# Shift and scale of the first norm: all four quarters of w_ada as matmul weights with two moving columns

## Chip, core and metric
One core of one Trainium2 chip. The metric is the device time of one execution in microseconds (us); of the kernel before, three runs took 3079.60, 3080.01 and 3080.32. Engines are named as in the profile: PE (TensorE matmul), PEld (its weight loads), DVE (VectorE), ACT (ScalarE), POOL (GpSimd), SP (SyncE, which here issues most transfers).

## What is computed
A block with attention, a gated linear recurrence and a convolutional feed-forward on 512 tokens of width 1024 with 256 context tokens, then four further layers. The change concerns its first lines:

```python
mod = jax.nn.silu(c) @ w_ada[layer] + b_ada[layer]
mod_c = jax.nn.silu(c_ctx) @ w_ada[layer] + b_ada[layer]
sh1, sc1, gt1, sh2, sc2, gt2 = jnp.split(mod[:, None, :], 6, axis=-1)
sh1c, sc1c, gt1c, sh2c, sc2c, gt2c = jnp.split(mod_c, 6, axis=-1)
h = modulate(rms_norm(x_lat, norm1_g[layer]), sh1, sc1)
hc = modulate(rms_norm(x_ctx, norm1_g[layer]), sh1c, sc1c)
```

with `modulate(h, shift, scale) = h * (1 + scale) + shift`. The projections q, kv and so on take `h` and `hc`.

## The kernel before
**Layout.** Activations lie with the channel on the partitions: eight blocks of 128 channels (KD = 8) by 512 tokens, and 256 more columns for the context. A shift or a scale is thus one column of 128 values for each block; `m01` holds them as [128, 8 blocks, token or context, shift or scale]. Inputs are fp32. Large products are made of three: weights and activations are split into a rounded high part and a rest (`whi`, `wlo`, `xh`, `xl`), and `mm3` issues high by high, high by rest and rest by high (lines 202, 203, 204).

**Where the work is.** `norm1` (from line 400) is the first stage of the program. `w_ada01` is the part of w_ada for shift and scale, stored as four quarters of 2 MB: quarter 0 is the shift of blocks 0 to 3, quarter 1 the scale of the same, quarter 2 shift and scale of blocks 4 and 5, quarter 3 of blocks 6 and 7. Each comes in two transfers (`adaw`, four buffers), each with four of the eight 128-row blocks of the contraction.

- *Quarters 0 and 1* (`ada`, `columns`). The weights of the array are the two silu vectors padded with zeros to 32 columns (`s2`), and the moving operand is w_ada, 512 columns: eight fp32 products a quarter (line 441) give a 32x512 row, ACT copies it out (444), and eight transposes (452) bring the rows into columns. DVE then adds the bias or scales (456 to 458).
- *Quarters 2 and 3* (`fetch`, `sums`). For each of the two vectors a weighted sum over the eight blocks is built on 128x512 tiles (`adas`): for the tokens on DVE (476), for the context by ACT (478) and POOL (479). Then a product with a column of ones sums over the partitions (483), 128x2 each.
- *The factors* (`factors`). The squares of x are summed over the blocks (292, 295 on ACT, 298 on DVE), `inv_rms` sums over the partitions (223) and makes 1/rms on DVE, `spread` makes a row of it over all partitions with two products (264), and ACT copies that out (266).
- *The products* (`first`). For each block k, x times the factor (502: two blocks on DVE, six on POOL), then `operand`: `xh` on ACT (508), a second copy `u` and the rest `xl` on DVE (510, 512, 513), both by the block's columns in `m01`; then 15 products of 512 columns into five banks (two for kv, three for q). Eight blocks make 120. The context follows with 48 products of 256 columns. After these come two panels `gq`, 24 products each, the first of them mixed in with the context before.

**What sets the order.** The program is written as one sequence. A scheduler then places the instructions, and each engine runs its own list in the order that it made; an engine that waits holds up all behind it. The places of the `next(...)` calls only suggest the order. SP issues transfers in its list's order too, and a raw panel (`wraw`) has three buffers.

`group` issues a row of matmuls as one accumulation in a bank:

```python
        ops = [self.nc.tensor.matmul(*o, start=i == 0, stop=i == last) for i, o in enumerate(ops)]
        for i in range(1, last + 1):
            self.after(ops[0], ops[i])
```

Of the kernel before, what the change touches and what calls it, by code (L numbers as in the profile page):

```python
# [155 lines left out]
class K:  # L156
# [214 lines left out]
    def silu_c(self, pool):  # L371
        nc = self.nc
        self.s2 = pool.tile([P, KD, 32], F32, name="s2")
        nc.vector.memset(self.s2, 0.0)
        nc.scalar.activation(self.s2[:, :, 0], self.v("c", 0, 8), AF.Silu)
        nc.scalar.activation(self.s2[:, :, 1], self.v("c_ctx", 0, 8), AF.Silu)
# [23 lines left out]
    def norm1(self, psp, psf, psb, evict_q, then):  # L400
# [3 lines left out]
        with self.pool(name="n1", bufs=1) as pool:  # L404
# [3 lines left out]
            def first(k):  # L408
# [10 lines left out]
                for t, a, b in ((0, 0, 256), (1, 256, 640)):  # L419
# [8 lines left out]
            row = self.wp.tile([P, PANEL], F32, tag="wraw", name=self.nm("row"),  # L428
                               bufs=self.raw_bufs)[:32, :].rearrange("p (q c) -> p q c", q=2)

            def ada(q):

                ps = psp.tile([P, 512], F32, tag="mm", name=self.nm("ps"))
                for h in range(2):
                    raw = pool.tile([P, 4, 512], F32, tag="adaw", name=self.nm("adaw"), bufs=4)
                    nc.sync.dma_start(raw, A["w_ada01"][q, h])
                    for k in ((range(4), range(4, 6)), (range(6, 8), ()))[q][h]:
                        nc.sync.dma_start(xa[:, k, :T], A["xa"][k, :, :T])
                    for i in range(4):
                        k = 4 * h + i  # L440
                        nc.tensor.matmul(ps[:32, :], self.s2[:, k, :], raw[:, i, :], start=k == 0, stop=k == KD - 1)
                    if h == 0:
                        yield 1
                nc.scalar.copy(row[:, q, :], ps[:32, :])
                yield 1

            def columns():

                for k in range(4):
                    for j in range(2):  # L450
                        o = (k * 2 + j) * 32
                        nc.tensor.transpose(fl[:, o:o + 32], row[:, j, k * P:(k + 1) * P], self.ident[:32, :32])
                f = fl[:, :256].rearrange("p (k j c) -> p k j c", j=2, c=32)
                cols = lambda v: v.rearrange("p (k o) -> p k o", o=1).to_broadcast([P, 4, 2])
                sc = m01[:, :4, :, 1]
                nc.vector.tensor_tensor(sc, f[:, :, 1, :2], cols(g[:, :4]), ALU.mult)
                nc.vector.tensor_tensor(sc, sc, cols(bg[:, :4]), ALU.add)
                nc.vector.tensor_tensor(m01[:, :4, :, 0], f[:, :, 0, :2], cols(self.v("b_ada", 0, 4)), ALU.add)

            def fetch(p):  # L460

                raws = []
                for h in range(2):
                    raws.append(pool.tile([P, 4, 512], F32, tag="adaw", name=self.nm("adaw"), bufs=4))
                    nc.sync.dma_start(raws[h], A["w_ada01"][p, h])
                return raws

            def sums(p, i, raws):

                t = pool.tile([P, 512], F32, tag=f"adas{i}", name=self.nm("adas"), bufs=2)  # L470
                for k in range(KD):
                    r, f = raws[k // 4][:, k % 4, :], self.s2[:, k, i:i + 1]
                    if k == 0:
                        nc.scalar.mul(t, r, f)
                    elif i == 0:
                        nc.vector.scalar_tensor_tensor(t, r, f, t, ALU.mult, ALU.add)
                    else:
                        nc.scalar.mul(r, r, f)
                        nc.gpsimd.tensor_tensor(t, t, r, ALU.add)
                yield 1  # L480
                o = 384 + ((p - 2) * 2 + i) * 8
                for c in range(4):
                    nc.tensor.matmul(fl[:, o + 2 * c:o + 2 * c + 2], t[:, c * P:(c + 1) * P], self.ones[:, 0:2],
                                     start=True, stop=True)
                ks = slice(2 * p, 2 * p + 2)
                sc = m01[:, ks, i, 1]
                nc.vector.tensor_tensor(sc, fl[:, o + 4:o + 8:2], g[:, ks], ALU.mult)
                nc.vector.tensor_tensor(sc, sc, bg[:, ks], ALU.add)
                nc.vector.tensor_tensor(m01[:, ks, i, 0], fl[:, o:o + 4:2], self.v("b_ada", 2 * p, 2), ALU.add)
# [25 lines left out]
            for _ in ada(0):  # L515
                pass
            a1 = ada(1)
            next(a1)
            r = factors(0, T)
            next(a1)  # L520
# [5 lines left out]
            raws = [fetch(2)]  # L526
            pans = [next(wf[0])]
            columns()
            next(wf[2])
            pkv = [psb.tile([P, 1024], F32, tag="big", name=self.nm("ps")) for _ in range(2)]  # L530
            pq = [psp.tile([P, 512], F32, tag="mm", name=self.nm("ps")) for _ in range(3)]
            for k in range(KD):
# [11 lines left out]
                if k == 0:  # L544
                    c2 = sums(2, 0, raws[0])
                    next(c2)
                    raws.append(fetch(3))
                    t2 = sums(2, 1, raws[0])
                    next(t2)
# [1245 lines left out]
```

## Time and profile before
| what | value |
|---|---|
| median of 3 runs | 3080.01 us |
| profiled execution | 3079.63 us |
| its span, first to last instruction | 3077.8 us |
| PE busy, share of the span | 2989.1 us, 97% |
| DVE, ACT, POOL busy | 70%, 48%, 17% |
| mean granted PE clock | 0.987 |
| chain that ended last | PE 78%, DVE 7%, ACT 2%, issue 2%, POOL 1% |

The profiled execution takes 1.83 us more than its span. The chain is followed back from the last instruction to what released it at each step. Busy matmuls overlap: a record's duration is longer than the distance to the next, so costs are read from the distance between starts. An fp32 product stands as two records, one of `xh` and its like as one. The granted clock is a share of 2.4 GHz; the levels met are 1.00 and 0.50.

### The profile page before, as it was taken

The page shows a single profiled execution, that of the slowest core. Times are in us where ns is not written, and L with a number is a line of the kernel's source. Part 1 is how long each engine was busy: PE and PEld are TensorE (multiplying, and loading weights), DVE is VectorE, ACT ScalarE, POOL GpSimd, SP SyncE. Part 2 cuts the span into 40 slices and gives each one's busy share as a digit, 9 for nine tenths or more (in the row PEclk, how much of TensorE's full clock was granted, in tenths as well). Part 3 has the DMA queues.
Part 4 walks back from the last instruction along what each step waited for, and adds up shares of the span by engine and source line. Part 5 has one row for each costly group of instructions (what it writes and reads, how often), then busy time and mean ns, then how long its engine had stood idle before and what let it go on. Part 6 is the DMA issues. An engine that isn't in the chain of part 4 may idle for free.

```text
span 3077.8 us, 42669 instructions
## 1 busy us (share of the span) xinstructions
PE 2989.1 (97%) x16044; PEld 2566.1 (83%) x16044; DVE 2159.4 (70%) x3596; ACT 1475.9 (48%) x2429; POOL 508.8 (17%) x453
## 2 busy tenths in 40 slices
PE   7999999989999999999999999999999999999998
PEld 4878778778888778999888999888899987789997
DVE  7858795689953985666845677765566788756766
ACT  5336653443333664444544445532444466644544
POOL 3212310110001211111201111210211122111112
PEclk8999999999999999999999999999999999999999
DMA  5671233523333435667524666623566654357664
GB/s 203 195 240 53 83 111 109 199 90 96 97 94 99 123 92 156 160 166 171 139 93 127 163 166 161 145 95 97 145 162 168 166 127 125 97 156 171 159 168 107
DMA packets 164271, 421.08 MB, mean 137 GB/s; under 512 B 18241, under 2 KB 24769, under 8 KB 163041
## 3 DMA queue, kind: packets, MB, share of 16 engines
q1 hardware_dynamic: 118000, 334.91, 34.5%
q0 software_dynamic: 36864, 67.13, 13.5%
q10 hardware_dynamic: 9200, 16.32, 1.6%
q8 instruction: 126, 2.06, 0.3%
q14 instruction: 81, 0.66, 0.1%
HBM read 398.10 MB, written 13.63 MB: 134 GB/s over the span
## 4 chain that ended last, share of the span: by engine, by line
PE 78%; DVE 7%; ACT 2%; issue 2%; POOL 1%; DMA 0%; SPq 0%; POOLq 0%; DVEq 0%; ACTq 0%
PE ps L334 20%; PE ps L202 18%; PE ps L204 18%; PE ps L203 18%; DVE wlo L188 1%; DVE xc L1264 1%; PE po L223 1%; DVE wlo L285 1%; PE pu L928 0%; DVE xc L1338 0%; PE pt L811 0%; DVE tg L1336 0%; PE ps L223 0%; ACT whi L186 0%; DVE x L1189 0%
## 5 line engine op out<-in xcount | busy, mean ns | idle before, releaser
L202 PE MATMUL ps<-xh,whi 128*128 128x512 f32 x2224 | 873.7, 394 | 11.4 <-ACT xh L508 6.6
L204 PE MATMUL ps<-xh,wlo 128*128 128x512 f32 x2224 | 873.1, 393 | 5.4 <-DVE wlo L188 4.6
L203 PE MATMUL ps<-xl,whi 128*128 128x512 f32 x2224 | 872.5, 392 | 3.1 <-DVE xl L513 3.1
L186 ACT CAST whi<-wraw 128x1024 fp32r<-128x1024 f32 (+2 forms) x267 | 265.1, 995 | 549.2 <-PE ps L203 383.7
L334 PE MATMUL ps<-hh,whi 128*128 128x256 f32 x1792 | 511.1, 285 | 5.1 <-DVE x L1189 5.1
L334 PE MATMUL ps<-hl,whi 128*128 128x256 f32 x1792 | 508.0, 283 | 0.0
L334 PE MATMUL ps<-hh,wlo 128*128 128x256 f32 x1792 | 504.2, 283 | 0.0
L202 PEld LDWEIGHTS ps<-xh,whi 128*128 128x128 f32 x2224 | 420.8, 189 | 99.7 <-ACT xh L508 6.8
L204 PEld LDWEIGHTS ps<-xh,wlo 128*128 128x128 f32 x2224 | 420.6, 189 | 96.6 <-DVE wlo L188 7.4
L203 PEld LDWEIGHTS ps<-xl,whi 128*128 128x128 f32 x2224 | 421.0, 189 | 90.1 <-DVE xl L513 4.6
L188 DVE TENSOR_TENSOR wlo<-wraw,whi 128x1024 fp32r<-128x1024 f32 (+2 forms) x257 | 300.2, 1168 | 186.9 <-ACT whi L186 185.4
L279 ACT CAST whi<-wraw 128x512 fp32r<-128x512 f32 (+2 forms) x400 | 232.7, 612 | 366.0 <-PE ps L203 231.6
L105 POOL DMA_DIRECT2D s<-in_w x256 | 223.9, 1038 | 1053.2 <-ACT s L116 513.5
L334 PEld LDWEIGHTS ps<-hh,whi 128*128 128x128 f32 x1792 | 343.4, 192 | 10.3 <-ACT whi L279 3.5
L334 PEld LDWEIGHTS ps<-hl,whi 128*128 128x128 f32 x1792 | 343.6, 192 | 0.7
L334 PEld LDWEIGHTS ps<-hh,wlo 128*128 128x128 f32 x1792 | 342.4, 192 | 0.0
L285 DVE TENSOR_TENSOR wlo<-wraw,whi 128x512 fp32r<-128x512 f32 (+2 forms) x400 | 264.1, 686 | 19.5 <-ACT whi L279 11.3
L1189 DVE TENSOR_TENSOR x<-x,ps 128x256 f32<-128x256 f32 x448 | 185.0, 417 | 114.8 <-PE ps L334 113.5
L279 ACT CAST whi<-s 128x512 fp32r<-128x512 f32 x256 | 153.4, 617 | 188.9 <-PE ps L334 147.7
L1178 DVE SCALAR_TENSOR_TENSOR H<-ps,rb 128x512 f32<-128x512 f32 x128 | 88.1, 691 | 177.6 <-PE ps L204 174.8
L298 POOL TENSOR_TENSOR acc_x<-acc_x,sq 128x512 f32<-128x512 f32 x54 | 79.2, 1467 | 651.6 <-ACT sq L295 650.9
L285 DVE TENSOR_TENSOR wlo<-s,whi 128x512 fp32r<-128x512 f32 x256 | 178.9, 715 | 10.4 <-ACT whi L279 1.2
(418 smaller groups left out, 4425.9 us busy)
## 6 DMA issues: line engine op xcount, KB each, us to landing
wraw<-in_w SPq DMA_DIRECT2D x192, 512.0 KB, 3.9
s<-in_w POOLq DMA_DIRECT2D x256, 256.0 KB, 6.5
s<-in_w SPq DMA_DIRECT2D x128, 256.0 KB, 5.0
wraw<-in_w_up SPq DMA_DIRECT2D x44, 512.0 KB, 3.4
wraw<-in_a_w_in SPq DMA_DIRECT2D x40, 512.0 KB, 3.5
wraw<-in_w_ada SPq DMA_DIRECT2D x32, 512.0 KB, 4.2
a<-in_w SPq DMA_DIRECT2D x64, 256.0 KB, 5.3
wraw<-in_w_in SPq DMA_DIRECT2D x29, 512.0 KB, 3.7
```

Of the source, the lines that this page charges most:

```text
L105: d = nc.gpsimd.dma_start(t, x, accum_op=ALU.add)
L186: nc.scalar.copy(hi[:, :n], raw[:, :n])
L188: e.tensor_tensor(lo[:, :n], raw[:, :n], hi[:, :n].bitcast(F32), ALU.subtract)
L202: mm(out, wh, xh, start=start, stop=False)
L203: mm(out, wh, xl, start=False, stop=False)
L204: mm(out, wl, xh, start=False, stop=stop)
L279: i = nc.scalar.copy(hi, src)
L285: e.tensor_tensor(lo, src, hi.bitcast(F32), ALU.subtract)
L298: (nc.vector if k == last else eng or nc.gpsimd).tensor_tensor(acc, acc, s, ALU.add)
L334: mm = lambda *o, **kw: self.nc.tensor.matmul(*o, skip_group_check=not start, **kw)
L1178: nc.vector.scalar_tensor_tensor(h, ps, 0.0, self.rb, ALU.max, ALU.mult)
L1189: nc.vector.tensor_tensor(x[:, n, :], x[:, n, :], ps, ALU.add if sign > 0 else ALU.subtract)
```

## The change
All four quarters go one way: w_ada's 128x128 blocks are the weights of the array and the two silu vectors are the moving operand, so that a product gives the 128x2 columns directly. A quarter is 8 x 4 = 32 fp32 products in one group (32 for each p, line 223 in the profile, since `group` records there). `s2` shrinks to two columns without the memset, and `row`, `columns`, `sums` and the tiles `adas` go. Quarters 2 and 3 are placed behind blocks 1 and 3 of the products, and all of `fetch` stands ahead of them.

```diff
-        self.s2 = pool.tile([P, KD, 32], F32, name="s2")
-        nc.vector.memset(self.s2, 0.0)
+        self.s2 = pool.tile([P, KD, 2], F32, name="s2")
...
-            def ada(q):
...
-                    for i in range(4):
-                        k = 4 * h + i
-                        nc.tensor.matmul(ps[:32, :], self.s2[:, k, :], raw[:, i, :], start=k == 0, stop=k == KD - 1)
...
-                nc.scalar.copy(row[:, q, :], ps[:32, :])
-            def columns():
...
-                for k in range(4):
-                    for j in range(2):
-                        o = (k * 2 + j) * 32
-                        nc.tensor.transpose(fl[:, o:o + 32], row[:, j, k * P:(k + 1) * P], self.ident[:32, :32])
...
-            def fetch(p):
+            def fetch(p, xs=((), ())):
...
                 raws = []
                 for h in range(2):
                     raws.append(pool.tile([P, 4, 512], F32, tag="adaw", name=self.nm("adaw"), bufs=4))
                     nc.sync.dma_start(raws[h], A["w_ada01"][p, h])
+                    for k in xs[h]:
+                        nc.sync.dma_start(xa[:, k, :T], A["xa"][k, :, :T])
                 return raws
-            def sums(p, i, raws):
...
-                    if k == 0:
-                        nc.scalar.mul(t, r, f)
-                    elif i == 0:
-                        nc.vector.scalar_tensor_tensor(t, r, f, t, ALU.mult, ALU.add)
-                    else:
-                        nc.scalar.mul(r, r, f)
-                        nc.gpsimd.tensor_tensor(t, t, r, ALU.add)
...
-                    nc.tensor.matmul(fl[:, o + 2 * c:o + 2 * c + 2], t[:, c * P:(c + 1) * P], self.ones[:, 0:2],
-                                     start=True, stop=True)
...
+            def ada(p, raws):
+
+                if p < 2:
+                    o, ps = 0, psp.tile([P, 512], F32, tag="mm", name=self.nm("ps"))
+                else:
+                    o, ps = 384 + 8 * (p - 2), fl
+                self.group([(ps[:, o + 2 * c:o + 2 * c + 2], raws[k // 4][:, k % 4, c * P:(c + 1) * P], self.s2[:, k, 0:2])
+                            for k in range(KD) for c in range(4)])
+                got = ps[:, o:o + 8].rearrange("p (c i) -> p c i", i=2)
+                cols = lambda v, n: v.rearrange("p (k o) -> p k o", o=1).to_broadcast([P, n, 2])
+
+                def shift(ks, v):
+                    nc.vector.tensor_tensor(m01[:, ks, :, 0], v, cols(self.v("b_ada", 0, 8)[:, ks], ks.stop - ks.start),
+                                            ALU.add)
+
+                def scale(ks, v):
+                    n, sc = ks.stop - ks.start, m01[:, ks, :, 1]
+                    nc.vector.tensor_tensor(sc, v, cols(g[:, ks], n), ALU.mult)
+                    nc.vector.tensor_tensor(sc, sc, cols(bg[:, ks], n), ALU.add)
+
+                if p < 2:
+                    (shift, scale)[p](slice(0, 4), got)
+                else:
+                    ks = slice(2 * p, 2 * p + 2)
+                    shift(ks, got[:, 0:2, :])
+                    scale(ks, got[:, 2:4, :])
...
-            for _ in ada(0):
-                pass
-            a1 = ada(1)
-            next(a1)
+            raws = [fetch(0, (range(4), range(4, 6)))]
+            raws.append(fetch(1, (range(6, 8), ())))
+            ada(0, raws[0])
             r = factors(0, T)
-            next(a1)
+            ada(1, raws[1])
             for k in range(KD):
                 scaled(k, r, 0, T, nc.vector if k < 2 else nc.gpsimd)
             wf = [first(k) for k in range(KD)]
             next(wf[0])
             next(wf[1])
-            raws = [fetch(2)]
+            raws.append(fetch(2))
             pans = [next(wf[0])]
-            columns()
             next(wf[2])
+            raws.append(fetch(3))
             pkv = [psb.tile([P, 1024], F32, tag="big", name=self.nm("ps")) for _ in range(2)]
             pq = [psp.tile([P, 512], F32, tag="mm", name=self.nm("ps")) for _ in range(3)]
...
                 if k == 0:
-                    c2 = sums(2, 0, raws[0])
-                    next(c2)
-                    raws.append(fetch(3))
-                    t2 = sums(2, 1, raws[0])
-                    next(t2)
-                if k == 1:
                     nc.sync.dma_start(xa[:, :, T:], A["xa"][:, :, T:].rearrange("k p t -> p k t"))
-                    next(c2, 0)
-                    c3 = sums(3, 0, raws[1])
-                    next(c3)
-                if k == 2:
-                    t3 = sums(3, 1, raws[1])
-                    next(t3)
-                if k == 3:
-                    next(c3, 0)
+                if k in (1, 3):
+                    ada(2 + k // 2, raws[2 + k // 2])
                 if k == 4:
                     rc = factors(T, TA)
-                if k == 6:
-                    next(t2, 0)
             for k in range(KD):
                 if k in (1, 3, 5):
                     evict_q(k // 2, pq[k // 2])
                 if k == 2:
                     first_panel = then()
-                if k == 4:
-                    next(t3, 0)
```

Below, `adaw` with a lower number is an earlier transfer. PE at the start of the program, before:

```order
L441 MATMUL ps_122<-adaw_123,s_95 32x512 x4
L441 MATMUL ps_122<-adaw_133,s_95 32x512 x4
L441 MATMUL ps_142<-adaw_143,s_95 32x512 x4
L223 MATMUL ada_117<-ones,acc_151 128x2 x4
L452 MATMUL ada_117<-ident,row_121 128x32
L441 MATMUL ps_142<-adaw_198,s_95 32x512 x3
L264 MATMUL psr_174<-rmsd_191,ones_r 128x512
L441 MATMUL ps_142<-adaw_198,s_95 32x512
L264 MATMUL psr_174<-rmsd_194,ones_r 128x512
L452 MATMUL ada_117<-ident,row_121 128x32 x7
L202 MATMUL ps_242<-xh,whi_222 128x512
```

and now:

```order
L223 MATMUL ps_136<-s_95,adaw_120 128x2 x16
L223 MATMUL ps_136<-s_95,adaw_126 128x2 x16
L223 MATMUL ada_116<-ones,acc_170 128x2 x4
L264 MATMUL psr_193<-rmsd_210,ones_r 128x512
L264 MATMUL psr_193<-rmsd_213,ones_r 128x512
L223 MATMUL ps_217<-s_95,adaw_130 128x2 x16
L223 MATMUL ps_217<-s_95,adaw_134 128x2 x16
L223 MATMUL ada_116<-s_95,adaw_264 128x2 x16
L202 MATMUL ps_282<-xh,whi_269 128x512
L202 MATMUL ps_283<-xh,whi_269 128x512
```

Quarter 0 is the first two rows, quarter 1 stands behind the factor's products, and the first half of quarter 2 (`adaw_264`) is ahead of the first product with `xh`.

DVE in the same stretch, at the sums of squares (298) and the factor (238), before:

```order
L298 TENSOR_TENSOR acc_151<-acc_151,sq_156 128x512
L298 TENSOR_TENSOR acc_151<-acc_151,sq_159 128x512
L298 TENSOR_TENSOR acc_151<-acc_151,sq_162 128x512
L298 TENSOR_TENSOR acc_151<-acc_151,sq_165 128x512
L298 TENSOR_TENSOR acc_151<-acc_151,sq_168 128x512
L298 TENSOR_TENSOR acc_151<-acc_151,sq_171 128x512
L238 TENSOR_SCALAR rmsw_180<-ada_117 128x4
```

and now:

```order
L298 TENSOR_TENSOR acc_170<-acc_170,sq_175 128x512
L298 TENSOR_TENSOR acc_170<-acc_170,sq_178 128x512
L450 TENSOR_TENSOR m_119<-ps_136,vecs 128x8
L298 TENSOR_TENSOR acc_170<-acc_170,sq_181 128x512
L298 TENSOR_TENSOR acc_170<-acc_170,sq_184 128x512
L298 TENSOR_TENSOR acc_170<-acc_170,sq_187 128x512
L298 TENSOR_TENSOR acc_170<-acc_170,sq_190 128x512
L238 TENSOR_SCALAR rmsw_199<-ada_116 128x4
```

The shift of quarter 0 (450), which reads what PE wrote, has come between the third and the fourth of the seven sums.

PE behind block 2 of the products (`whi_321` is its and block 3's panel), now:

```order
L202 MATMUL ps_286<-xh,whi_321 128x512
L203 MATMUL ps_286<-xl,whi_321 128x512
L204 MATMUL ps_286<-xh,wlo_323 128x512
L223 MATMUL ada_116<-s_95,adaw_278 128x2 x16
L223 MATMUL ada_116<-s_95,adaw_280 128x2 x16
L202 MATMUL ps_282<-xh,whi_385 128x512
L203 MATMUL ps_282<-xl,whi_385 128x512
```

Both halves of quarter 3 stand ahead of block 3; the second half of quarter 2 is likewise ahead of block 2.

## Rows read from the trace of the kernel before
**Rows 1.** Page, busy us, share and instructions of each engine.
```profile
PE 2989.1 (97%) x16044; PEld 2566.1 (83%) x16044; DVE 2159.4 (70%) x3596; ACT 1475.9 (48%) x2429; POOL 508.8 (17%) x453
```

**Rows 2.** Windows of 10 us: PE, PEld, DVE, ACT, POOL busy, granted clock, DMA share, GB/s.
```profile
30.00:40.00 10.00, 5.48 (x12) 3.93 (x13) 9.96 (x11) 5.50 (x9) 7.29 (x6) 0.50 0.69 257
40.00:50.00 10.00, 7.48 (x29) 5.88 (x29) 9.36 (x8) 4.96 (x9) 6.86 (x6) 0.84 0.13 35
50.00:60.00 10.00, 9.03 (x29) 7.01 (x29) 9.23 (x11) 5.60 (x9) 8.39 (x6) 0.72 0.12 33
```

**Rows 3.** Waits, 30 to 70 us: total us, times, longest.
```profile
ACT adaw L478 <- DVE adas L476: 10.1, 9, 2.3
...
PE ps L202 <- ACT xh L508: 6.6, 2, 5.5
```

**Rows 4.** Tile adas: duration ns min/median/max, first and last start.
```profile
L476 DVE SCALAR_TENSOR_TENSOR adas<-adaw,s,adas x14: 737/1663/1789, 30.7 to 58.6; 128x512 f32<-128x512 f32 x14
L479 POOL TENSOR_TENSOR adas<-adas,adaw x14: 1268/1520/2389, 35.0 to 62.8; 128x512 f32<-128x512 f32 x14
```

**Rows 5.** Timeline of PE, the marks of the stage: start us, duration us, engine, line.
```profile
31.69 2.50 PE L202 MATMUL ps<-xh,whi 128*128 128x512 f32 x5 [5.49 <-ACT xh L508]
...
81.54 0.28 PE L202 MATMUL ps<-ch,whi 128*128 128x256 f32 x1
...
82.26 0.28 PE L202 MATMUL ps<-ch,whi 128*128 128x256 f32 x1
...
102.66 1.39 PE L223 MATMUL psr<-ones,kacc 128*128 128x2 f32 x12
```

**Rows 6.** Timeline of PE, 32 thin records between dense products.
```profile
513.05 0.40 PE L204 MATMUL ps<-oh,wlo 128*128 128x512 f32 x1
...
515.39 1.84 PE L223 MATMUL psr<-ones,e 128*128 128x2 f32 x16
517.10 1.93 PE L223 MATMUL psr<-ones,bc 128*128 128x2 f32 x16
518.88 0.48 PE L202 MATMUL ps<-oh,whi 128*128 128x512 f32 x1
...
523.30 0.39 PE L202 MATMUL ps<-oh,whi 128*128 128x512 f32 x1
```

**Rows 7.** Timeline of PE, thin products and the rise behind them.
```profile
48.75 1.87 PE L483 MATMUL ada<-ones,adas 128*128 128x2 f32 x8 [2.52 <-DVE adas L476]
50.48 0.77 PE L203 MATMUL ps<-xl,whi 128*128 128x512 f32 x1
...
55.32 0.97 PE L202 MATMUL ps<-xh,whi 128*128 128x512 f32 x3
```

**Rows 8.** Windows, as rows 2, at the clock's low level.
```profile
50.00:55.00 5.00, 5.00 (x14) 4.03 (x15) 4.34 (x8) 3.42 (x6) 3.62 (x3) 0.50 0.23 66
519.80:523.00 3.20, 3.20 (x10) 2.42 (x9) 2.17 (x9) 0.00 (x0) 0.00 (x0) 0.50 0.24 87
```

**Rows 9.** Timeline, 6 to 24 us.
```profile
6.59 12.74 PE L441 MATMUL ps<-adaw,s 128*32 128x512 f32 x24 [6.59 <-DMA adaw<-in_w_ada]
...
8.26 0.18 PEld L441 LDWEIGHTS ps<-adaw,s 128*32 128x32 f32 x1 [0.68 <-issue]
...
9.12 0.18 PEld L441 LDWEIGHTS ps<-adaw,s 128*32 128x32 f32 x1 [0.68 <-issue]
...
11.87 0.11 PEld L441 LDWEIGHTS ps<-adaw,s 128*32 128x32 f32 x1 [0.32 <-DMA adaw<-in_w_ada]
12.30 0.11 PEld L441 LDWEIGHTS ps<-adaw,s 128*32 128x32 f32 x1 [0.32 <-issue]
...
17.07 1.49 DVE L298 TENSOR_TENSOR acc<-acc,sq 128x512 f32<-128x512 f32 x2 [2.52 <-ACT sq L295]
...
19.26 1.05 PE L223 MATMUL ada<-ones,acc 128*128 128x2 f32 x8
...
23.45 0.49 PE L264 MATMUL psr<-rmsd,ones_r 128*128 128x512 f32 x1
```

More of the change, by code (lines that the diff above doesn't have):

```diff
@@ L427, in norm1 @@
             m01 = pool.tile([P, KD, 2, 2], F32, name="m01")
-            row = self.wp.tile([P, PANEL], F32, tag="wraw", name=self.nm("row"),
-                               bufs=self.raw_bufs)[:32, :].rearrange("p (q c) -> p q c", q=2)
-            def ada(q):
[L433 to L438, printed above, removed]
-                    for i in range(4):
-                        k = 4 * h + i
-                        nc.tensor.matmul(ps[:32, :], self.s2[:, k, :], raw[:, i, :], start=k == 0, stop=k == KD - 1)
-                    if h == 0:
-                        yield 1
-                nc.scalar.copy(row[:, q, :], ps[:32, :])
-                yield 1
-            def columns():
-                for k in range(4):
-                    for j in range(2):
-                        o = (k * 2 + j) * 32
-                        nc.tensor.transpose(fl[:, o:o + 32], row[:, j, k * P:(k + 1) * P], self.ident[:32, :32])
[L453 to L458, printed above, removed]
-            def fetch(p):
+            def fetch(p, xs=((), ())):
                 raws = []
@@ L465, in fetch @@
                     nc.sync.dma_start(raws[h], A["w_ada01"][p, h])
-                return raws
-            def sums(p, i, raws):
-                t = pool.tile([P, 512], F32, tag=f"adas{i}", name=self.nm("adas"), bufs=2)
-                for k in range(KD):
-                    r, f = raws[k // 4][:, k % 4, :], self.s2[:, k, i:i + 1]
-                    if k == 0:
-                        nc.scalar.mul(t, r, f)
-                    elif i == 0:
-                        nc.vector.scalar_tensor_tensor(t, r, f, t, ALU.mult, ALU.add)
-                    else:
-                        nc.scalar.mul(r, r, f)
-                        nc.gpsimd.tensor_tensor(t, t, r, ALU.add)
-                yield 1
-                o = 384 + ((p - 2) * 2 + i) * 8
-                for c in range(4):
-                    nc.tensor.matmul(fl[:, o + 2 * c:o + 2 * c + 2], t[:, c * P:(c + 1) * P], self.ones[:, 0:2],
-                                     start=True, stop=True)
[L485 to L489, printed above, removed]
```

## The prediction
> **What bounds the kernel now.** I read the page first: TensorE (PE) is busy 97% of the span [rows 1], so a microsecond that PE loses or gains anywhere is nearly a microsecond of the total, as long as it is on PE's own path. The windows of the stage that the change touches come next [rows 2]: from 30 to 60 us PE is busy 5.5 to 9.0 of each 10 us and has a granted clock of 0.50 to 0.84, while VectorE (DVE) is busy 9.2 to 10. The reader is to see two losses there, idle PE and slow PE. The waits of this stretch say who is late [rows 3]: ScalarE (ACT) waits 10.1 us in all for the DVE that builds the weighted sums `adas`, PE 6.6 us in two waits for the normalized block `xh`. The tile view says why: the 14 DVE steps on `adas` have a median of 1663 ns where the shortest takes 737, and beside them POOL does 14 additions of 1520 [rows 4]. Last, the timeline of PE gives the marks against which I count: first product of `first` at 31.69 us, last group over the 512 tokens done at 81.54, and the end of the two gq panels at 102.66 [rows 5].
>
> **What is removed.** The zeroed 32-column s2, 16 wide products, two row copies, eight transposes, and for quarters 2 and 3 the DVE steps (14, some 23 us), the POOL additions (14, some 21 us) and ACT's scalings. Their benefit is that DVE, ACT and POOL are free from 30 to 62 us, so that PE should wait for none of them there. That is the hope, and I grant it in full below: in my sum PE never waits for an operand after its first product.
>
> **What is added, and its price.** Every quarter is now 32 products with a 128x128 block of w_ada as weights and two moving columns. The trace has this very form, L223 and L483: each fp32 product is two records. At full clock 16 records take 517.10 - 515.39 = 1.71 us, 0.107 each [rows 6]; at half clock eight take 50.48 - 48.75 = 1.73, 0.216 each [rows 7]. A quarter is 64 records: 6.8 us at full clock, 13.8 at half. Which clock it gets decides the case.
>
> **The clock.** The stretch in [rows 6] shows it at its plainest: 32 such records follow dense 512-column products without a gap and are followed by dense products. At 519.8 the granted clock is 0.50 all the same, the lower level of 1.2 GHz [rows 8], and full spacing is back only at 523.30. PE had not idled before it fell: dense products, 3.5 us of two-column ones, four dense ones. For the rise, [rows 7]: from 48.75 PE has eight records of this kind, then dense 512-column products from 50.48; the window 50 to 55 is at 0.50 throughout [rows 8] and the quick spacing comes within the row at 55.32, five us after the dense products began. I take from this that a stream of two-column products neither raises the clock nor holds it. The Trainium skill, page "TensorE: Matmul & The Clock Gate", part 1 on the clock gate, says otherwise in one respect: the warm-up is a budget of time under sustained work, whatever the number and spacing of the matmuls. By that rule a gapless quarter would warm itself and the sum would be rival B's; [rows 6] disagree, since 3.5 us of gapless thin products were followed by the low level. I sum by the rows.
>
> **The sum, step by step.** (1) Quarter 0 starts at 6.59 as before. PE is slow there already before: its weight loads stand 0.86 us apart at 8.26 and 9.12 and 0.43 at 11.87 and 12.30, where dense work has gone ahead [rows 9]. The second block's transfer is there at 11.87 and holds nothing up. 64 x 0.216 = 13.8: it ends at 20.4. (2) In DVE's order the shift of quarter 0 now stands ahead of the last four sums of squares, so these wait for PE. Two take 1.49 us [rows 9]; four take 3.0 and the shift 0.16: 23.6, where before the last two began at 17.07 and ended at 18.56. (3) The factors: eight records at 0.216 end at 25.3. Before, from the end of these (19.26 + 1.05) to the first `psr` at 23.45 were 3.1 us, with one 0.4 us weight split in between that now comes later: 2.7, so 28.0, and 1.1 for two `psr` products of 512 columns at 0.43 and the end of the second: 29.1. (4) Quarter 1, 13.8: 42.9. Only now can DVE finish the scale columns of blocks 0 to 3. (5) The order has the first half of quarter 2 ahead of the first product: 6.9, so the first product is at 49.8, and what it needs has been made meanwhile. Before it was at 31.69. **PE is 18.1 us late there.**
>
> (6) From there to the end of the last 512-token group: 120 products at 0.234 (ten from 513.05 to 515.39 [rows 6]) are 28.1. The first five us run at half clock, about 11.6 products at 0.43 (ten in the 3.2 us from 519.8, [rows 8], with its ends cut), which costs 2.3. The second half of quarter 2 is 32 x 0.107 = 3.4, and the fall behind it costs what it cost in [rows 6]: twelve products in 523.30 - 518.88 = 4.4 us instead of 2.8, so 1.6. Quarter 3 is 6.8 to 13.8; half of it at each level gives 10.3. The slow products behind it cost again 2.3. The four records and two 256-column products of the context's factor: 0.7. Sum 48.7, so the stage ends at 98.5. Before it took 81.54 - 31.69 = 49.9 with all its waits; so the freed engines give back 1.2 us only, and PE is 17.0 late.
>
> (7) The context groups and the two gq panels: 48 products at 0.12 (six from 81.54 to 82.26, [rows 5]) and 48 at 0.23 are 16.8; before they took 102.66 - 81.54 = 21.1, with thin products, waits and a slow stretch among them. This gives back 4.3. **PE is 12.7 us late at the mark of 102.66**, and behind that mark the order is the same. The profiled execution took 3079.63 us, 1.83 more than its span and 0.4 under the median of 3080.01. I round the loss down to 12, since some of the waits behind the mark can soak up a little: 3092.
>
> No term is left for the transfers: the last blocks of w_ada are issued when quarter 1's buffers come free, by 43, and quarter 3 comes at some 67. The two row copies and the memset were beside other work and give nothing.
>
> Bounds: with all of quarter 3 at half clock (+3.5) and the two warm-ups as long as from 48.75 to 55.32, 6.6 us instead of 5 (+1.5), the loss is 17.7. With quarter 3 wholly at full clock (-3.5) and no loss behind it (-2.3), it is 6.9; if waits behind the mark, none of which I have priced, give back 3 more, 3.9.
>
> **Rivals.** B, the other sign, **faster**: thin products count as work, and the clock rises about five us after 6.59 and stays. Then quarter 0 is 21 records at half and 43 at full clock, 6.59 + 4.6 + 4.6 = 15.8; the sums end as before at 18.6; factors 0.9 + 2.7 + 1.1 give 23.3; quarter 1 ends at 30.1, the half of quarter 2 at 33.5; the products 28.1 + 3.4 + 6.8 + 0.7 end at 72.5, and with 16.8 the mark comes at 89.3, 13.4 us early: 3066. This decides itself at quarter 1: if its 64 records take 7 us, B holds; at 14 it is dead. For it speaks the Trainium skill's rule named above; against it [rows 6, 7]. Chance 0.09.
>
> C, **no difference that can be told**: the early quarters run at half clock as I say, but later thin stretches, between dense products, do not make it fall. Then 1.6, 3.5 and 2.3 drop out: 12.7 - 7.4 = 5.3 us, 3085. Against it speak [rows 6], but the fall there came after a whole 32 records, and where the stretch lies may matter. Chance 0.14.
>
> D, **slower still**: quarter 3's columns stand ahead of the operands of blocks 3 to 7 on DVE, and ACT's casts of late weight panels are queued behind those operands; if PE runs out after quarter 3, as in the shorter of the two waits for `xh` in [rows 3] (6.6 - 5.5 = 1.1 us), some three or four times, it adds 4: 3096. The freed DVE speaks against it. Chance 0.07.
>
> A change that does not do what it says is hardly open: the order shows the 128 products and none of the old sums.
>
> **How the numbers follow.** A, my forecast, has 0.70: 3092, own range 3084 to 3098. The range for 8 in 10 takes in A's bounds, D and most of C: 3082 to 3099; B and the rest of C stay out. About 0.2% (6 us) is what a measurement of this kernel can tell from no change. Slower by more than that: 0.63 of A, 0.07 of D and 0.02 of C, 0.72. Within: 0.07 of A and 0.12 of C, 0.19. Faster: B, 0.09.
>
> **What would show it.** Right: the 64 records of each of the first two quarters last 13 to 14 us at a spacing of 0.21; the first product stands near 50 us; DVE's last four sums of squares begin behind the end of quarter 0; PE hardly waits between 50 and 98; the second gq panel ends near 115. Wrong: the first product before 40 us, or records 0.107 apart in a quarter with no dense product ahead of it. If the first product is late as told and the time is not, a wait behind 102.66 has swallowed the loss.

## The result and the profile after

The changed kernel takes 3098.86 us (median of 4 runs, 3098.06 to 3101.31); the ratio to the kernel before is 1.0064, interval 1.0052 to 1.0076. It is slower, as forecast, but by more than forecast: the ratio times 3080.01 is 3099.7 us, just above the upper end of the range, where 3092 was named. The profiled execution took 3098.30 us with a span of 3096.3.

The page's engine line answers to [rows 1]:

```profile
PE 3015.7 (97%) x16228; PEld 2606.7 (84%) x16228; DVE 2131.9 (69%) x3575; ACT 1464.1 (47%) x2409; POOL 486.1 (16%) x439
```

DVE, ACT and POOL have lost 28, 12 and 23 us of work, PE has gained 27 us and 184 instructions. The work was moved to the engine that bounds the kernel.

The windows that answer to [rows 2], in their columns:

```profile
30.00:40.00 10.00, 10.00 (x49) 10.00 (x48) 0.00 (x0) 0.00 (x0) 7.29 (x6) 1.00 0.29 105
40.00:50.00 10.00, 10.00 (x47) 9.90 (x47) 5.76 (x12) 5.05 (x8) 0.00 (x0) 1.00 0.63 219
50.00:60.00 10.00, 10.00 (x42) 8.13 (x40) 0.00 (x0) 0.00 (x0) 0.00 (x0) 1.00 0.26 91
```

PE, idle for 8 of these 30 us before, is now busy in all of them; DVE, busy for 28.6 of them before, is busy for 5.8. The clock column is no guide here: it reads 1.00 up to 61 us, where the record has its first fall (0.74 from 61 to 62, 0.50 from 62 to 63), although the records up to 54.6 us stand as far apart as at the low level. Up to a record's first fall the level has to be read from the distance between records, as below. Of the waits of [rows 3] and the tiles of [rows 4] none is left.

The timeline of PE, the marks that answer to [rows 5] (start us, duration us, engine, line; in brackets the idle time before and what ended it):

```profile
6.61 13.78 PE L223 MATMUL ps<-s,adaw 128*128 128x2 f32 x64 [6.61 <-DMA adaw<-in_w_ada]
23.64 1.86 PE L223 MATMUL ada<-ones,acc 128*128 128x2 f32 x8 [3.25 <-DVE acc L298]
27.80 1.39 PE L264 MATMUL psr<-rmsd,ones_r 128*128 128x512 f32 x2 [2.29 <-DVE rmsd L260]
28.99 13.65 PE L223 MATMUL ps<-s,adaw 128*128 128x2 f32 x64
42.49 6.96 PE L223 MATMUL ada<-s,adaw 128*128 128x2 f32 x32
49.32 2.48 PE L202 MATMUL ps<-xh,whi 128*128 128x512 f32 x5
...
54.87 0.40 PE L203 MATMUL ps<-xl,whi 128*128 128x512 f32 x1
...
58.81 4.38 PE L223 MATMUL ada<-s,adaw 128*128 128x2 f32 x32
63.05 0.77 PE L202 MATMUL ps<-xh,whi 128*128 128x512 f32 x1
...
69.02 11.17 PE L223 MATMUL ada<-s,adaw 128*128 128x2 f32 x64
80.06 0.77 PE L202 MATMUL ps<-xh,whi 128*128 128x512 f32 x1
...
100.78 0.28 PE L202 MATMUL ps<-ch,whi 128*128 128x256 f32 x1
...
106.14 0.39 PE L203 MATMUL ps<-cl,whi 128*128 128x256 f32 x1 [0.85 <-DVE cl L487]
...
108.87 0.39 PE L203 MATMUL ps<-cl,whi 128*128 128x256 f32 x1 [1.77 <-DVE cl L487]
...
109.78 0.63 PE L202 MATMUL ps<-xh,whi 128*128 128x512 f32 x1
...
112.74 0.40 PE L203 MATMUL ps<-xl,whi 128*128 128x512 f32 x1
...
122.06 1.39 PE L223 MATMUL psr<-ones,kacc 128*128 128x2 f32 x12
```

Windows of PE over the second half of quarter 2 and behind, and quarter 3 and behind (PE busy, granted clock, DMA share, GB/s):

```profile
63.05:68.30 5.25, 5.25 (x13) 0.50 0.00 0
69.02:80.06 11.04, 11.04 (x66) 0.62 0.00 0
80.06:85.30 5.24, 5.24 (x13) 0.50 0.23 64
```

What the reader is to see: quarters 0 and 1 take 13.8 and 13.7 us for 64 records, 0.214 each, half rate from the first to the last (the price of [rows 7], against 0.107 of [rows 6]). The first product stands at 49.32 instead of 31.69. Quarter 3 takes 11.0 us, and for more than 5 us behind it the granted clock is 0.50; the same stands behind the second half of quarter 2. The first `psr` behind the panels (`psr<-ones,kacc`, the last mark of [rows 5]; below it is called the mark) is at 122.06 instead of 102.66, 19.4 us late; the span's end is 18.5 late. So almost all of the loss is made in the first 122 us and carried to the end.

### The profile page after: what moved, and what is told of

The parts are those of the page before. It is cut to its first block, busy times and chain, and to the rows that moved or that the text cites. A ratio compares the mean times of both kernels' runs of the same rounds, so it can differ in the third digit from the quotient of the medians.

```text
span 3096.3 us, 42963 instructions
## 1 busy us (share of the span) xinstructions
PE 3015.7 (97%) x16228; PEld 2606.7 (84%) x16228; DVE 2131.9 (69%) x3575; ACT 1464.1 (47%) x2409; POOL 486.1 (16%) x439
## 4 chain that ended last, share of the span: by engine, by line
PE 77%; DVE 8%; ACT 2%; issue 2%; POOL 1%; DMA 0%; POOLq 0%; DVEq 0%; ACTq 0%; SPq 0%
PE ps L334 20%; PE ps L202 18%; PE ps L204 18%; PE ps L203 18%; DVE wlo L188 1%; DVE xc L1221 1%; DVE wlo L285 1%; PE po L223 1%; DVE xc L1295 1%; PE pu L885 0%; PE ps L223 0%; PE pt L768 0%; DVE tg L1293 0%; DVE x L1146 0%; ACT whi L186 0%
```

## Experiments

The theory (A in the expectations): two-column (thin) products neither raise PE's clock nor hold it up, so that they run at half rate themselves and slow what stands behind them. Its rivals: the late pair does not move the clock (W), the clock falls for the weight loads or the fp32 form and not for the columns (W2), and the loss is one of order (O); and a theory on the last part of the loss, the context stage (L). First product and mark are from the profiled executions, ratios from the timed runs against the kernel before on the same chip.

| run | first product | first `psr` | ratio (interval) |
|---|---|---|---|
| kernel before | 31.69 | 102.66 | 1 |
| changed kernel | 49.32 | 122.06 | 1.0064 (1.0052 to 1.0076) |
| 1 late pair thin alone | 37.60 | 106.88 | 1.0017 (1.0008 to 1.0027) |
| 2 early pair thin alone | 44.41 | 115.14 | 1.0042 (1.0030 to 1.0054) |
| 3 late pair spread | 44.38 | 136.44 | 1.0102 (1.0089 to 1.0115) |
| 4 quarter 1 ahead of the factors | 43.82 | 115.53 | 1.0050 (1.0038 to 1.0062) |
| 5 q evictions later | 49.27 | 117.61 | 1.0068 (1.0054 to 1.0082) |
| 6 all four wide | 32.22 | 97.74 | 0.9990 (0.9982 to 0.9999) |
| 7 wide, 128 weight columns | 31.37 | 95.67 | 0.9991 (0.9981 to 1.0000) |
| 8 128 moving columns | 35.38 | 94.78 | 0.9980 (0.9970 to 0.9990) |
| 9 64 moving columns | 43.72 | 105.62 | 1.0007 (0.9997 to 1.0017) |
| 10 128, quarter 1 first | 28.24 | 92.57 | 0.9977 (0.9967 to 0.9986) |
| 11 two columns, same order | 44.72 | 120.56 | 1.0060 (1.0046 to 1.0073) |
| 12 128 early, two late | 34.42 | 103.69 | 1.0008 (0.9998 to 1.0018) |

**Runs 1 and 2: one pair at a time.** Run 1 puts quarters 0 and 1 back:

```diff
-            raws = [fetch(0, (range(4), range(4, 6)))]
-            raws.append(fetch(1, (range(6, 8), ())))
-            ada(0, raws[0])
+            for _ in ada_w(0):
+                pass
+            a1 = ada_w(1)
+            next(a1)
             r = factors(0, T)
-            ada(1, raws[1])
+            next(a1)
```

> Quarters 0 and 1 as in the kernel before (512 moving columns, transposes), quarters 2 and 3 as in the changed kernel. Theory A (two-column products neither raise PE's clock nor hold it, so the second pair costs PE some 24 us of thin and slowed products, less the waits for DVE that it removes): first product near 35 us (half of quarter 2 stands ahead of it), last 512-token product near 87, the first psr near 108; total about 3086, between 3083 and 3089. Rival W (the thin products of the late pair cost only their 13.7 us at full clock, and the early pair is the whole loss): 3075 or less. If the late pair is the whole loss: 3095 or more.

Run 2 keeps them as changed and puts `sums` of quarters 2 and 3 back, with their places.

> Quarters 0 and 1 as in the changed kernel, quarters 2 and 3 by the weighted sums of the kernel before. Theory A: the first two quarters run at half clock, 13.6 us each, first product near 43 us instead of 31.7; but DVE, ACT and POOL build the sums of quarter 2 in that time, so PE waits less afterwards: last 512-token product at 81 to 86, total 3080 to 3085, far less than the 11 us by which the first product is late. If the early pair is the whole loss: 3090 or more.

Run 1 came out as theory A had it (1.0017, some 5 us). Run 2 did not: 1.0042, some 13 us, where 0 to 5 were expected. I had let DVE build the sums of quarter 2 while PE worked on quarter 1. In DVE's list they stand behind the first operands, which wait for quarter 1's scale columns, so they begin at 46.1 us where they began at 30.7 before, and PE waits 6.1 us for them all the same. The two pairs add up: 13 and 5 of the 20 us.

**Run 3: the thin products spread.** One product of quarters 2 and 3 behind each dense product of blocks 0 to 3, order pinned:

```diff
+            def block(ops, thin, last):
+                for o in ops:
+                    d = nc.tensor.matmul(*o[:3], start=o[3], stop=o[4])
+                    if last[0] is not None:
+                        self.after(last[0], d)
+                    last[0] = d
+                    if thin is not None:
+                        t = next(thin)
+                        if t is not None:
+                            self.after(last[0], t)
+                            last[0] = t
```

> The changed kernel with the 64 thin products of quarters 2 and 3 put one behind each dense product of blocks 0 to 3, in a fixed order; same work, and no half quarter ahead of the first product. Theory A: first product near 44 us; the dense products between keep the clock up, thin records come 0.107 apart, no stretch at half clock after the first rise: last 512-token product near 90 instead of 100.8, total 3087 to 3090. If the mixture does not raise the clock (thin products count against it): blocks 0 to 3 take 55 us, total 3110 or more. Rival W (clock not moved by the thin products): only the half quarter ahead of the first product is saved, 5 us, total 3094.

The timeline of PE in run 3 (L482 and L552 are the dense products, L472 the thin ones):

```profile
47.38 0.77 PE L482 MATMUL ps<-xh,whi 128*128 128x512 f32 x1
47.95 0.42 PE L472 MATMUL ada<-s,adaw 128*128 128x2 f32 x2
48.24 0.77 PE L482 MATMUL ps<-xl,whi 128*128 128x512 f32 x1
...
96.66 1.27 PE L472 MATMUL ada<-s,adaw 128*128 128x2 f32 x6
97.79 0.77 PE L552 MATMUL ps<-xh,whi 128*128 128x512 f32 x1
98.36 0.63 PE L552 MATMUL ps<-xl,whi 128*128 128x512 f32 x1
...
100.78 0.39 PE L552 MATMUL ps<-xl,whi 128*128 128x512 f32 x1
101.01 0.39 PE L552 MATMUL ps<-xh,wlo 128*128 128x512 f32 x1
```

A dense product and a thin one take 0.86 us together where 0.45 is their price at full clock (0.234 and twice 0.107): half rate, from the first pair at 44.38 to the last thin record, 53 us in which PE is never idle after one short wait at 45.65. This is read from the spacing alone, since the clock column of this run has its first fall only behind 120 us; but once only dense products follow (97.79), the spacing stays at 0.43 and then falls to 0.23 within 3 us, so the level was low until then. So what I expected by theory A (the mixture keeps the clock up) is wrong, its core is not: in these 53 us the clock did not come up, with a dense product between each two thin ones. Rival W of the expectations is out, and so is rival B of the prediction, that thin products count as work. The Trainium skill, page "TensorE: Matmul & The Clock Gate", part 1, has the warm-up as a budget of time under sustained work, whatever the number and spacing of the matmuls. These 53 us disagree, and so do the 13.8 us of quarter 0.

**Run 4: order of quarter 1.**

```diff
             ada(0, raws[0])
+            ada(1, raws[1])
             r = factors(0, T)
-            ada(1, raws[1])
```

> The changed kernel with quarter 1 written ahead of the factors, so that half of it stands ahead of the sums over the partitions and half between them and the psr products; work and clock as in the changed kernel. Theory A's second step (PE idles 3.25 and 2.29 us for the factors only because of the order): first product near 43 instead of 49.3, total near 3093. If the order does not matter because the chain of x times factor and xh (5.5 us of waiting before) ends last anyway: first product at 47 or later, total 3097 to 3099.

First product at 43.82, first `psr` 6.5 us earlier: the idle time of PE before the factors was a matter of order, as step 2 said. In the total it is some 4 us (1.0050 against 1.0064; the intervals overlap).

**Run 5: the context stage.** In the changed kernel PE waits for `cl` at 106.14 and 108.87. DVE at that time:

```profile
104.35 1.40 DVE L1509 SCALAR_TENSOR_TENSOR ql<-ps,vecs,qh 128x512 fp32r<-128x512 f32 x2
105.67 0.41 DVE L487 TENSOR_TENSOR cl<-u,ch 128x256 fp32r<-128x256 f32 x1
106.00 1.21 DVE L188 TENSOR_TENSOR wlo<-wraw,whi 128x1024 fp32r<-128x1024 f32 x1
107.14 0.68 DVE L1515 TENSOR_TENSOR qacc<-qacc,sq 128x512 f32<-128x512 f32 x1
107.74 0.74 DVE L1509 SCALAR_TENSOR_TENSOR ql<-ps,vecs,qh 128x512 fp32r<-128x512 f32 x1
108.40 0.41 DVE L487 TENSOR_TENSOR cl<-u,ch 128x256 fp32r<-128x256 f32 x1
```

The last two `cl` stand behind the q evictions (1509), a panel's split (188) and a sum of squares (1515). The edit moves `evict_q` behind the loop over the context:

```diff
-                if k in (1, 3, 5):
-                    evict_q(k // 2, pq[k // 2])
...
+            for k in range(3):
+                evict_q(k, pq[k])
```

> The changed kernel with the three q evictions written behind the context loop instead of inside it, so that on DVE all eight context operands cl stand ahead of them; the same work. Theory L (the last 4.5 us of the loss come from the context stage: PE waits 0.85 and 1.77 us for cl behind the evictions on DVE, and the clock falls after it): the waits for cl fall under 0.5 us, the panels behind them run at full clock from the start, first psr near 117.5 instead of 122.06, total 3093 to 3095. Rival: the wait is only moved (cl is late because x times the factor on POOL is late, or the panel's split, now queued behind the evictions, holds PE up): first psr at 120 or later, total 3097 to 3100.

Timeline of PE, then of ACT, in run 5:

```profile
117.61 1.39 PE L223 MATMUL psr<-ones,kacc 128*128 128x2 f32 x12
...
121.55 0.50 PE L202 MATMUL ps<-xh,whi 128*128 128x512 f32 x1 [1.65 <-ACT whi L186]
```

```profile
120.45 1.04 ACT L186 CAST whi<-wraw 128x1024 fp32r<-128x1024 f32 x1 [6.69 <-DMA wraw<-in_w_in]
```

Up to the mark theory L holds to 0.1 us: 117.61, 4.45 earlier. In the total nothing of it is seen: 1.0068 against 1.0064 (a gain of 4.5 us lies at the edge of what the two intervals can rule out). What PE won it met again in the next panel: ACT has waited 6.69 us for the panel's transfer, PE 1.65 for ACT. In the changed kernel ACT ends that split at 120.05 and PE comes to this point at 124.21, so nobody waits there. Between 115 and 270 us PE waits 6.7 us for such splits (`whi`, line 186) in run 5, 4.3 in the changed kernel. This accounts for some 2.4 of the 4.45 us. Counted at the same products of both profiled executions, the lead is 4.45 us at the mark, 2.93 at the first `pt` (135.02 in the changed kernel), 1.26 at the fourth (248.96) and gone at 493. So it is lost piece by piece over the stages behind; what takes the part beyond the 2.4 is not settled, and executions of one kernel differ by several us (run 5's from 3096.22 to 3101.96).

**Runs 6 and 7: the other form for all.** Run 6 is the kernel before with `wide` for quarters 2 and 3 in place of `sums`: silu vectors as 32 weight columns, 512 columns of w_ada moving, then a row copy and four transposes a quarter, in a PSUM bank that is free during the token blocks.

```diff
+            def wide(p, raws):
+                ps = pkv[p - 2][:, 512:1024]
+                row = pool.tile([32, 512], F32, tag="row2", name=self.nm("row"), bufs=2)
                 for k in range(KD):
...
+                    nc.tensor.matmul(ps[:32, :], self.s2[:, k, :], raws[k // 4][:, k % 4, :], start=k == 0, stop=k == KD - 1)
```

> All four quarters in the form that the kernel before has for quarters 0 and 1: the padded silu vectors (32 columns) as weights and 512 columns of w_ada moving, 16 records a quarter, then a copy on ACT and four transposes for each late quarter; no weighted sums on DVE and POOL and no thin products. Theory A (thin products are what costs; the freed DVE, ACT and POOL are a real gain): first product near 31.7 as before, the late pair costs 32 records of 0.234 and eight transposes, 8.4 us, last 512-token product near 74 instead of 81.5 and 100.8, first psr near 95, total near 3072, between 3069 and 3076. Rival (products with 32 weight columns hold the clock down as well): up to 12 us more, 3078 to 3086.

Run 7 pads the weights of all four quarters to 128 columns (`s2p[:, k, :]`, the rest zero).

> As the run with all four quarters wide, with the silu vectors padded with zeros to 128 weight columns instead of 32 in all four; the results are the same. If the clock goes by how much of the array a product uses (512 moving columns of 32 weight columns never raised it between 6.6 and 25 us in the kernel before): the records of quarter 0 come 0.234 apart instead of 0.43 from some 12 to 14 us on, the clock is up or rises sooner at the first product, total 2 to 5 us under the wide run. If the weight columns do not matter: the same time as the wide run within 1 us.

The timeline of PE in run 6:

```profile
47.87 7.05 PE L472 MATMUL ps<-adaw,s 128*32 128x512 f32 x16
54.85 0.50 PE L202 MATMUL ps<-xh,whi 128*128 128x512 f32 x1
55.19 0.40 PE L203 MATMUL ps<-xl,whi 128*128 128x512 f32 x1
```

Sixteen records take 7.0 us, 0.44 each, at a granted clock of 1.00, and the dense products behind them run at full clock too (0.34 and then 0.23 apart): 0.44 is what an fp32 record with 512 columns costs here at full clock, not 0.23, and a wide quarter costs PE as much as a thin one at full clock (6.8). My 8.4 us for the late pair should have been some 15. Even so the first `psr` is 9.1 us earlier than in run 1, whose early pair is the same and whose late pair is thin. The wide form leaves no slow stretch behind it: the granted clock is 1.00 from 44 to 67 us. The weight columns (run 7) made no difference that can be told. What I wrote ahead of run 7 misread [rows 9]: the 0.43 between the loads at 11.87 and 12.30 is the full-clock price of this form, and the 0.86 at 8.26 is the low level. The wide early quarters of the kernel before thus came to full clock by 11.87 us, some five us after their start; the changed kernel gave this up.

**Runs 8 to 12: the moving columns.** The decisive edit, here with 128: the moving operand is padded with zeros, all else stays.

```diff
+            s2p = pool.tile([P, KD, 128], F32, name="s2p")
+            nc.gpsimd.memset(s2p, 0.0)
+            nc.vector.tensor_copy(s2p[:, :, :2], self.s2)
...
-                    o, ps = 384 + 8 * (p - 2), fl
-                self.group([(ps[:, o + 2 * c:o + 2 * c + 2], raws[k // 4][:, k % 4, c * P:(c + 1) * P], self.s2[:, k, 0:2])
+                    ps = pkv[p - 2][:, 512:1024]
+                self.group([(ps[:, 128 * c:128 * c + 128], raws[k // 4][:, k % 4, c * P:(c + 1) * P], s2p[:, k, :])
```

> The changed kernel with the moving operand padded with zeros from two columns to 128, the same 32 products a quarter and the same weight loads; the outputs of the late pair go to a free PSUM bank, by which the half quarter ahead of the first product moves behind block 1. Theory A (the clock follows the columns that PE streams, not how busy it is with weight loads): the clock rises some five us into quarter 0, which ends near 16 instead of 20.4; quarters 2 and 3 take 6.8 us each and nothing slow stands behind them; first product between 32 and 40, first psr between 96 and 107, total 3074 to 3084. Rival W2 (the clock falls because of the weight loads or the fp32 form of these products): clock as in the changed kernel, quarters at 13.6 us, first product near 44, total 3092 or more. If a record with 128 columns costs up to 0.21 us at full clock, theory A's times are 7 us later for each quarter that runs at full clock.

> As the run with 128 moving columns, with 64. Theory A says only that it lies between two and 128 columns: either the early stage looks like the 128-column run (first product before 40) or like the changed kernel (near 44), and the total goes with it, 3074 to 3084 or 3090 and more.

Run 10 is run 8 with the edit of run 4:

> As the run with 128 moving columns, with quarter 1 written ahead of the factors (half of it ahead of the sums over the partitions, half between them and psr). Theory A: PE no longer waits for the factors with quarter 1 still to do, first product near 32 as in the kernel before, and it never waits for the weighted sums that the kernel before has: last 512-token product near 77, first psr near 96, total 3070 to 3077. Rival W2: first product near 43, total 3090 or more.

The new PSUM bank also changes PE's order. Run 11 is the control, the same edit with two columns; run 12 has 128 in the early pair and two in the late one.

> Control for the padded runs: two moving columns, but the late pair's outputs in the PSUM bank that the padded runs use, so that PE's order is theirs (quarter 2 behind blocks 0 and 1, quarter 3 behind blocks 2 and 3, no half quarter ahead of the first product). Theory A (columns, not order): quarters 0 and 1 take 13.6 us each, first product near 44, each late quarter 11 us with 2.5 us of slow products behind it, first psr at 120 to 124, total 3096 to 3101, no better than the changed kernel. Rival O (the padded runs gained by the order alone): first psr at 95 to 106, total 3085 or less.

> 128 moving columns in quarters 0 and 1, two in quarters 2 and 3, in the same order. Theory A: early stage as with 128 columns throughout (first product near 35); each late quarter takes 11 us instead of 7.2 and leaves 2.5 us of slow products behind it, so first psr near 107 instead of 94.8, total 3084 to 3088. If two-column products between dense ones cost nothing but their records: 3073 to 3076.

PE's quarters and the mark, run 8 (128 columns):

```profile
7.27 9.28 PE L223 MATMUL ps<-s2p,adaw 128*128 128x128 f32 x64 [7.27 <-DMA adaw<-in_w_ada]
...
23.67 9.52 PE L223 MATMUL ps<-s2p,adaw 128*128 128x128 f32 x64
35.38 1.20 PE L202 MATMUL ps<-xh,whi 128*128 128x512 f32 x4 [2.19 <-ACT xh L485]
...
42.42 7.31 PE L223 MATMUL ps<-s2p,adaw 128*128 128x128 f32 x64
...
56.56 7.31 PE L223 MATMUL ps<-s2p,adaw 128*128 128x128 f32 x64
...
94.78 1.39 PE L223 MATMUL psr<-ones,kacc 128*128 128x2 f32 x12
```

run 9 (64 columns):

```profile
6.97 13.88 PE L223 MATMUL ps<-s2p,adaw 128*128 128x64 f32 x64 [6.97 <-DMA adaw<-in_w_ada]
...
53.34 7.25 PE L223 MATMUL ps<-s2p,adaw 128*128 128x64 f32 x64
```

run 11 (two columns, same order):

```profile
6.88 13.79 PE L223 MATMUL ps<-s2p,adaw 128*128 128x2 f32 x64 [6.88 <-DMA adaw<-in_w_ada]
...
53.20 9.16 PE L223 MATMUL ps<-s2p,adaw 128*128 128x2 f32 x64
...
72.02 10.77 PE L223 MATMUL ps<-s2p,adaw 128*128 128x2 f32 x64
```

run 12 (128 early, two late):

```profile
41.45 10.67 PE L223 MATMUL ps<-s2p,adaw 128*128 128x2 f32 x64
...
52.56 0.63 PE L203 MATMUL ps<-xl,whi 128*128 128x512 f32 x1
52.99 0.63 PE L204 MATMUL ps<-xh,wlo 128*128 128x512 f32 x1
```

With 128 columns the late quarters take 7.3 us, 0.114 a record at full clock against 0.107 for two columns: the padding costs next to nothing, and the granted clock is 1.00 from 42.42 to 70 us. Quarter 0 ends at 16.5 instead of 20.4, as expected; quarter 1, behind PE's waits for the factors, takes 9.5, so it too begins at the low level and leaves it. The mark, 94.78, comes a little ahead of the 96 I named as the earliest, and the total is 0.998 of before. With two columns in the same order it is 1.0060: order alone gives 1.5 us at the mark and nothing that can be told in the total, so rival O is out, and with the weight loads and the fp32 form the same in both, rival W2 too. Run 12 divides the gain: two columns in the late pair alone put the mark from 94.78 to 103.69, and the products behind them are 0.43 apart again (52.56, 52.99). I expected 107; the total, 1.0008, is a little better than the 3084 to 3088 I gave. With 64 columns the early pair stays at half rate, like two columns, and the late pair, which comes at full clock, stays at full clock, like 128; so the total, 1.0007, does not go with the early stage as I had expected. Runs 8 and 10 beat both kernels by a little, 0.2% under the kernel before, with intervals that end below 1: 3073.61 and 3074.09 us, against 3080.32 for the kernel before on their chip. The order of run 10, worth 2.2 us at the mark, cannot be told from run 8 in the total.

## Why the prediction was right, and where it was wrong

**Step 1, the price and the clock of the early pair: right.** 0.107 at full and 0.216 at half clock were the two prices; the quarter ended at 20.39 (20.4 forecast). That no quarter there comes to full clock was the choice that decided the case. Runs 8 and 11 differ in the moving columns alone, 128 against two, with the same 64 records and the same weight loads, and quarter 0 takes 9.28 us in one and 13.79 in the other. What rival B priced, early quarters that come to full clock, is seen in run 8 with 128 columns, though not all of it: quarter 0 to 16.5 (15.8), quarter 1 in 9.5 us (7), mark at 94.8 (89.3).

**Steps 2 to 5: right.** Sums of squares held up by `shift` until 23.64 (23.6), first factor product 27.80, quarter 1 to 42.6 (42.9), first product 49.32 (49.8).

**Step 6: 2.8 us too small, over 51.5 us.** Forecast 48.7 from the first product to the last group. Quarter 3 took 11.0 instead of 10.3, the second half of quarter 2 4.2 instead of 3.4, block 2 behind it 6.0 instead of 5.1: the fall came earlier and the low level lasted longer than in [rows 6], on which I had costed it. There the clock fell 4.4 us after the first thin record and was low for 3.4 us; here it fell 2.7 us after the first record of each stretch, at 61.5 and 71.7, and was low for 6.8 and 13.6 us. The mechanism was right, the size was taken from one stretch. Rival C is out: the later thin stretches made the clock fall.

**Step 7 is the step that failed.** "This gives back 4.3": it gave back nothing, 21.3 us (100.78 to 122.06) against the 21.1 of before. I had counted 48 and 48 products at full pace, and said of the whole that PE never waits for an operand after its first product. It waits twice for `cl`, 2.9 us beyond the normal spacing, because DVE's list has the evictions and a split ahead of the last two operands; and behind these waits the clock is low until 112.7, 1.6 us more. Together 4.5. In the kernel before such waits stand behind 82.26 [rows 5] too, but a little later `gq` products lie between the context's and fill the time; in the changed order they come after it, from 109.78 on. PE in the kernel before:

```profile
83.35 0.38 PE L203 MATMUL ps<-cl,whi 128*128 128x256 f32 x1 [0.81 <-DVE cl L513]
...
88.44 0.63 PE L202 MATMUL ps<-xh,whi 128*128 128x512 f32 x1
```

I had looked at DVE's list where the sums of squares stand, not here. The bounds of the prediction, a loss of 17.7 us at worst, had room for step 6 and none for this. Run 5 takes the waits away and has the 4.45 us back at the mark, so the mechanism is shown there. For the total it is not shown: run 5 has lost its lead by 493 us, and why it keeps none of it stays open.

**The rounding: right in size.** I took 0.7 off for waits behind the mark that soak up some of the loss. They took 0.9 (19.4 to 18.5). That it fits so well is in part luck: the same stretch took the whole 4.45 us that run 5 had won. With the two steps above this makes the sum: 12.7 + 2.8 - 0.5 (first product earlier) + 4.5 - 0.9 is 18.6; measured in the spans 18.5. Rival D's waits after quarter 3 did not come: PE has no idle time between 49.32 and 105 us. That step 7 cost about as much as D's 4 us is chance.

## What to carry to other kernels

In this kernel, which PE bounds, a product had two prices: the time of its records, and what the clock did in and behind it. By the first, records with two and with 128 moving columns are nearly alike at full clock (0.107 and 0.114 us); by the second the two forms lie 25.8 us apart at the mark (120.56 and 94.78). Where such a thin form is wanted, time it beside the same form padded with zeros, as in run 8, and look at the spacing of the products behind. When work is taken off other engines in favour of PE, go through their instruction lists at every later stage where PE is fed, not only where the change is.

## What the runs showed that I had not expected

That a dense product between each two thin ones does not bring the clock up in 53 us (run 3). That the same 64-column records run at half rate for 13.9 us when they come at the low level and at full rate for 7.25 us when they come at the high one (run 9). That 128 moving columns cost 0.114 us a record against 0.107 for two, and 512 columns in fp32 0.44 at full clock (runs 6 and 8).
